# One encoder layer on one core: down projections in turn, h through DRAM everywhere, x in small pieces, paired 64-row logits

## The chip, the cores and the metric

The kernel runs on one core of a Trainium2 chip. The metric is the device time of one execution in microseconds. A core has a matrix engine (TensorE, PE in the rows, with its weight loads as PEld), a vector engine (VectorE, DVE), a scalar engine (ScalarE, ACT), a general engine (GpSimd, POOL) and a sync engine (SyncE, SP) that here issues most DMAs. Matrix results land in PSUM banks of 128 partitions by 512 fp32; everything else is held in SBUF, and weights come from device memory.

## What is computed

256 tokens of width 2048 go through one layer; all weights are fp32. The parts that the change touches are the two SwiGLU feed-forward blocks, the differential attention and the token indexer:

```python
x <- LN(alpha*x + 0.5*SwiGLU_1(x))
x <- LN(alpha*x + W_o[g_A*(DiffAttn(x) W_A) + g_B*(DSA(x) W_B)])
x <- LN(alpha*x + MemCrossAttn(x, mem))
x <- LN(alpha*x + 0.5*SwiGLU_2(x))

def _swiglu(x, w_gate, w_up, w_down):            # 2048 -> 5632 -> 2048
    return (jax.nn.silu(x @ w_gate) * (x @ w_up)) @ w_down
logits = einsum('bthcd,bshcd->bhcts', q, k)      # DiffAttn: 8 heads, c = 2 components of 64
attn = p[:, :, 0] - lam * p[:, :, 1]
head_scores = relu(einsum('bthd,bsd->bths', iq, ik))   # indexer: 16 heads of 64
```

## The kernel before

Every fp32 operand is split into a rounded part and a remainder (`split`, lines 169 to 171: ACT casts `hi`, DVE subtracts to get `lo`), and each product is three matmuls, hi·hi, hi·lo, lo·hi (`mm3`, lines 173 to 176). Weights come in units of 128 x 1024 fp32 (512 KB, two contraction tiles of 512 columns). One unit serves two halves of the tokens (t = 0, 1), so a unit is 12 matmuls of 512 columns. `Feed` holds the plan of all units in the order of use: `load` (line 179) issues the DMA on SP's queue into one of RAW = 4 raw buffers, `split_unit` splits it into one of the slots, several units ahead of PE, and `pull` hands it to the product. `product` runs the units of one 512-column chunk into two PSUM banks (`acc`, 4 of them, taken in turn) and calls `tasks.tick()` after each unit. A task is a generator that runs to its next `yield` at each tick: smaller work is written between the units in this way, and what it writes on each engine stands in that place of the engine's queue.

`ffn` (line 484) runs over groups of FFN chunks, (0,4), (4,8) and (8,11). For each chunk it makes the gate product, `silu` on ACT, the up product, and spawns a task that forms h = 0.5·silu·up and transposes it into `hh` and `hl`. After the chunks of a group come four down products (n = 0 to 3), which take the h of the group's chunks as the stationary side, in the order of the chunks, two units to a chunk.

For all chunks but the last of an FFN the task is `h_bounced` (line 496): DVE transposes 32 x 32 blocks of h, POOL's queue issues eight small DMAs into `h_dram` and two back into `hnat`, and BOUNCE = 5 ticks later ACT and DVE split the result into `hh` and `hl`. For the last chunk, 10, it is `h_task` (line 489), which transposes with eight PE matmuls against `ident` (`blocks_T`, line 337).

At the start, two warm-up matmuls of zeros run (line 557). `x` arrives transposed in four pieces of 512 KB (`x_pieces`), which stand in the plan ahead of units 0, 2, 4 and 6 of the first gate chunk and use the raw buffers. All of the first gate product runs before the first up product.

`diff_head` makes the logits of its two components one after the other, and `index_task` those of two heads per tick: each is six matmuls on 64 rows (`logits`, and lines 791 to 799), three of 128 columns and three of 256, and the two of a pair lie in rows 0 to 63 and 64 to 127 of the array and in PSUM banks of their own (`tp`, 4 of them).

Of the kernel before, what the change touches and what calls it, by code (L numbers as in the profile page):

```python
# [16 lines left out]
P = 128  # L17
T = 256
# [27 lines left out]
BOUNCE = 5  # L46
# [38 lines left out]
class Feed:  # L85


    def __init__(self, load, split):
        self.load, self.split = load, split
        self.plan, self.nth, self.order = [], [], []  # L90
        self.loaded, self.ready = [], {}
        self.nsplit = self.pulled = 0
        self.slots = {}
        self.busy = False

    def add(self, key, src, width=UNIT, into=None, cut=1):
        self.nth.append(len(self.order))
        if into is None:
            self.order.append(len(self.plan))
        self.plan.append((key, src, width, into, cut))  # L100

    def _load(self):
        i = len(self.loaded)
        if i < len(self.plan):
            _, src, width, _, cut = self.plan[i]
            self.loaded.append(self.load(src, width, cut))
# [4 lines left out]
    def _split(self):  # L111
        i = self.nsplit
        while len(self.loaded) < min(len(self.plan), i + RAW):
            self._load()
        _, _, width, into, cut = self.plan[i]
# [7 lines left out]
        if len(self.loaded) < min(len(self.plan), self.nsplit + RAW):  # L123
            self._load()
# [26 lines left out]
def tile_encoder_layer(ctx, tc, a, out):  # L151
# [27 lines left out]
    def load(src, width, cut):  # L179
        raw = wraw.tile([P, UNIT], F32, name="raw")  # L180
        w = width // cut
        for i in range(cut):
            nc.sync.dma_start(raw[:, i * w:(i + 1) * w], src[:, i * w:(i + 1) * w])
# [4 lines left out]
    def split_unit(raw, width, into, cut, slot):  # L188
        if into is not None:
            hi, lo = into()  # L190
            raw = raw.rearrange("p (k t) -> p k t", t=T)
            w = 4 // cut
# [20 lines left out]

    def plan(w, n, kts, each=None):
        for i in range(0, len(kts), KT):
            if each is not None:
                each(i // KT)
            feed.add((w, n, kts[i][1] // KT), a[w][n, kts[i][1] // KT], cut=1 if feed.order else 2)
# [6 lines left out]

    def plan_ffn(pre, each=None):
        for c0, c1 in FFN_GROUPS:
            for c in range(c0, c1):
                plan(pre + "_w_gate", c, dense(KD), each if c == 0 else None)
# [4 lines left out]
    def x_pieces(src, box):  # L234
        def piece(i):
            def into():
                xT = box[0]
                return xT[:, 0, 4 * i:4 * i + 4, :], xT[:, 1, 4 * i:4 * i + 4, :]
            feed.add(None, a[src][:, i * 4 * T:(i + 1) * 4 * T], UNIT, into, cut=1 if feed.plan else 2)
        return piece  # L240

    xbox, membox = [None], [None]
    xp, mp = x_pieces("xT", xbox), x_pieces("memT", membox)
    plan_ffn("ffn1", lambda u: u % 2 == 0 and xp(u // 2))
# [23 lines left out]
    for n in range(4):  # L268
        plan("w_mix_out", n, dense(KD), (lambda u: u % 2 == 0 and mp(u // 2)) if n == 3 else None)
# [70 lines left out]
    def transposed(src, hi, lo, width=NCOL):  # L340

        p = blocks_T(src, width)[:, :width]
        split(hi, lo, p.rearrange("p (b t) -> p b t", t=P) if len(hi.shape) == 3 else p)

# [137 lines left out]


    def ffn(pre, pool, y, xT, sts, lead, end):

        for gi, (c0, c1) in enumerate(FFN_GROUPS):
            hT = []

            def h_task(s, u, hh, hl):
# [8 lines left out]
            def h_bounced(s, u, hh, hl):  # L498

                h = [pool.tile([P, NCOL], F32, name="hnat", bufs=3) for _ in range(2)]  # L500
                via = dram.tile([P, 2, 4, P], F32, name="h_dram", bufs=4)
                for t in range(2):
                    nc.vector.scalar_tensor_tensor(h[t], s[t], 0.5, u[t], op0=ALU.mult, op1=ALU.mult)
                yield
                for t in range(2):
                    nc.vector.transpose(s[t].rearrange("p (g b i) -> p g b i", b=4, i=32),  # L506
                                        h[t].rearrange("p (b g i) -> p g b i", b=4, i=32))
                    for q in range(4):
                        nc.gpsimd.dma_start(via[:, t, q].rearrange("(g i) c -> i g c", i=32),  # L509
                                            s[t][32 * q:32 * q + 32].rearrange("i (g c) -> i g c", g=4))  # L510
                for t in range(2):
                    nc.gpsimd.dma_start(h[t].rearrange("p (q c) -> p q c", q=4), via[:, t])
                for _ in range(BOUNCE):
                    yield
                for t in range(2):
                    sl = slice(t * P, (t + 1) * P)
                    split(hh[:, :, sl].rearrange("p b (q j) -> p b q j", j=32),
                          hl[:, :, sl].rearrange("p b (q j) -> p b q j", j=32),
                          h[t].rearrange("p (q b j) -> p b q j", b=4, j=32))

            for c in range(c0, c1):
                g = product(x_lhs(xT), pre + "_w_gate", c, dense(KD), lead=lead if c == 0 else 0)
                s = [pool.tile([P, NCOL], F32, name="silu", bufs=2) for _ in range(2)]
                for t in range(2):
                    nc.scalar.activation(s[t], g[t], AF.Silu)
                u = product(x_lhs(xT), pre + "_w_up", c, dense(KD))
# [11 lines left out]
            for n in range(4):  # L538
# [13 lines left out]
    with more_slots("wx1", MORE[0]), tc.tile_pool(name="ffn1", bufs=1) as pool:  # L552
# [6 lines left out]
        xT = xbox[0] = new_xT()  # L559
# [597 lines left out]
```

## Time and profile before

| | us |
|---|---|
| median of three runs | 2259.17 (2258.37 to 2260.03) |
| the profiled execution, its own time | 2260.71 |
| its span, first to last instruction | 2258.9 |
| PE busy | 2237.8, 99% of the span, 10248 matmuls |
| DVE, ACT, POOL busy | 1308.0, 1035.9, 131.5 |
| DMA | 458.26 MB, mean 203 GB/s |
| mean granted clock of TensorE | 0.998 |

A busy PE is counted from the start of a matmul to its modelled end, and neighbouring matmuls overlap: 512-column matmuls last 0.39 us by the record and start 0.23 us apart. Lost PE time is therefore read from the distance between starts, not from the busy share. In a timeline each row gives the start, the time covered, engine, line, operation, written and read tiles, shapes and count; the bracket gives the engine's idle time before it and what ended that.

### The profile page before, as it was taken

Reading aid. Unit: us, or ns where it says so; the run is one execution under the profiler, and the core shown is the slowest. Engines: PE = TensorE matmul, PEld = TensorE weight load, DVE = VectorE, ACT = ScalarE, POOL = GpSimd, SP = SyncE. Lnnn points to the kernel's source line nnn. Section 1 sums busy time; section 2 is a strip of 40 time slices with the busy share of each in tenths; the row PEclk is TensorE's granted clock in tenths of the full one; section 3 lists DMA queues with packets and bytes.
Section 4 is the critical chain, followed back from the end, with each engine's and each line's share of the span. In section 5 each row is a group of like instructions: output and inputs, shape, how many; then the busy total and the mean of one; then the engine's idle time right before and its main releaser. Section 6 shows DMA issues by size and latency. Waiting matters only on the chain.

```text
span 2258.9 us, 27277 instructions
## 1 busy us (share of the span) xinstructions
PE 2237.8 (99%) x10248; PEld 1850.0 (82%) x10248; DVE 1308.0 (58%) x1498; ACT 1035.9 (46%) x1317; POOL 131.5 (6%) x236
## 2 busy tenths in 40 slices
PE   9999999999999999999999999999999999999997
PEld 7888888888888888888888888878888888888886
DVE  6555555554556666685655556777555455554554
ACT  5443344444443555655544444655444344434442
POOL 0100000100000000000000000000000001100100
PEclk9999999999999999999999999999999999999999
DMA  8877677766665655445567667557776666766762
GB/s 272 315 236 212 190 210 215 213 207 195 212 209 168 209 159 165 151 147 170 183 193 207 202 224 263 174 168 227 221 251 207 194 213 212 230 192 191 221 198 91
DMA packets 128916, 458.26 MB, mean 203 GB/s; under 512 B 16704, under 2 KB 16832, under 8 KB 127632
## 3 DMA queue, kind: packets, MB, share of 16 engines
q1 hardware_dynamic: 119520, 431.02, 62.2%
q0 software_dynamic: 9264, 25.51, 3.4%
q8 instruction: 80, 1.31, 0.2%
q14 instruction: 52, 0.43, 0.1%
HBM read 441.78 MB, written 14.68 MB: 202 GB/s over the span
## 4 chain that ended last, share of the span: by engine, by line
PE 94%; DMA 2%; issue 1%; DVE 1%; ACT 1%; POOL 0%; POOLq 0%; SPq 0%; DVEq 0%; ACTq 0%
PE acc L174 30%; PE acc L176 30%; PE acc L175 30%; PE tp L337 2%; DMA hnat<-h_dram 1%; DMA h_dram<-silu 1%; PE tp L174 1%; PE tp L175 1%; PE tp L176 0%; DMA raw<-in_ffn_w_gate 0%; ACT whi L170 0%; DVE wlo L171 0%; POOL h_dram L509 0%; DVE y L479 0%; ACT me L1010 0%
## 5 line engine op out<-in xcount | busy, mean ns | idle before, releaser
L171 DVE TENSOR_TENSOR wlo<-raw,whi 128x1024 fp32r<-128x1024 f32 (+1 forms) x787 | 958.3, 1222 | 811.3 <-ACT whi L170 808.7
L170 ACT CAST whi<-raw 128x1024 fp32r<-128x1024 f32 (+1 forms) x787 | 824.1, 1051 | 932.5 <-PE acc L176 874.2
L174 PE MATMUL acc<-whi,xT 128*128 128x512 f32 x2176 | 853.8, 392 | 1.7 <-ACT whi L170 1.7
L176 PE MATMUL acc<-whi,xT 128*128 128x512 f32 x2176 | 848.3, 390 | 0.0
L175 PE MATMUL acc<-wlo,xT 128*128 128x512 f32 x2176 | 848.2, 390 | 0.0
L174 PEld LDWEIGHTS acc<-whi,xT 128*128 128x128 f32 x2176 | 409.2, 188 | 87.1 <-ACT whi L170 3.3
L176 PEld LDWEIGHTS acc<-whi,xT 128*128 128x128 f32 x2176 | 409.0, 188 | 86.0
L175 PEld LDWEIGHTS acc<-wlo,xT 128*128 128x128 f32 x2176 | 409.4, 188 | 84.4 <-DVE wlo L171 0.9
L174 PE MATMUL acc<-whi,hh 128*128 128x512 f32 x704 | 274.9, 390 | 2.3 <-ACT hh L170 2.3
L176 PE MATMUL acc<-whi,hl 128*128 128x512 f32 x704 | 274.4, 390 | 0.0
L175 PE MATMUL acc<-wlo,hh 128*128 128x512 f32 x704 | 274.0, 389 | 0.0
L174 PEld LDWEIGHTS acc<-whi,hh 128*128 128x128 f32 x704 | 132.1, 188 | 30.9 <-ACT hh L170 4.0
L176 PEld LDWEIGHTS acc<-whi,hl 128*128 128x128 f32 x704 | 132.1, 188 | 29.1 <-DVE hl L171 1.7
L175 PEld LDWEIGHTS acc<-wlo,hh 128*128 128x128 f32 x704 | 132.2, 188 | 27.3
L509 POOL DMA_DIRECT2D h_dram<-silu x160 | 87.2, 553 | 1077.0 <-DVE silu L506 1027.2
L174 PE MATMUL acc<-whi,ring 128*128 128x512 f32 x144 | 56.7, 394 | 0.0
L176 PE MATMUL acc<-whi,ring 128*128 128x512 f32 x144 | 56.1, 390 | 0.0
L175 PE MATMUL acc<-wlo,ring 128*128 128x512 f32 x144 | 56.1, 389 | 0.0
L479 DVE SCALAR_TENSOR_TENSOR y<-y,acc 128x512 f32<-128x512 f32 x64 | 42.2, 679 | 17.3 <-PE acc L176 17.3
L669 ACT ACTIVATE e<-e,nm 128x128 f32<-128x128 f32 (+1 forms) x48 | 21.5, 448 | 45.7 <-DVE nm L668 44.8
L170 ACT CAST hh<-hnat 128x512 fp32r<-128x512 f32 x40 | 24.8, 621 | 37.7 <-DMA hnat<-h_dram 34.8
L171 DVE TENSOR_TENSOR hl<-hnat,hh 128x512 fp32r<-128x512 f32 x40 | 27.4, 691 | 25.2 <-ACT hh L170 25.2
(200 smaller groups left out, 1136.6 us busy)
## 6 DMA issues: line engine op xcount, KB each, us to landing
raw<-in_ffn_w_up SPq DMA_DIRECT2D x176, 512.0 KB, 4.4
raw<-in_ffn_w_down SPq DMA_DIRECT2D x176, 512.0 KB, 4.2
raw<-in_ffn_w_gate SPq DMA_DIRECT2D x175, 512.0 KB, 4.3
raw<-in_w_in SPq DMA_DIRECT2D x88, 512.0 KB, 3.6
raw<-in_w_gate SPq DMA_DIRECT2D x64, 512.0 KB, 4.1
raw<-in_w_mix_out SPq DMA_DIRECT2D x32, 512.0 KB, 4.4
h_dram<-silu POOLq DMA_DIRECT2D x160, 64.0 KB, 4.4
hnat<-h_dram POOLq DMA_DIRECT2D x40, 256.0 KB, 5.3
```

The source lines that it names most:

```text
L170: nc.scalar.copy(hi, src)
L171: nc.vector.tensor_tensor(lo, src, hi.bitcast(F32), ALU.subtract)
L174: nc.tensor.matmul(dst, lh, rh, start=start, stop=False)
L175: nc.tensor.matmul(dst, lh, rl, start=False, stop=False)
L176: nc.tensor.matmul(dst, ll, rh, start=False, stop=stop)
L337: nc.tensor.transpose(p[:, b * P:(b + 1) * P], src[:, b * P:(b + 1) * P], ident)
L479: nc.vector.scalar_tensor_tensor(c, c, scale, d, op0=ALU.mult, op1=ALU.add)
L509: nc.gpsimd.dma_start(via[:, t, q].rearrange("(g i) c -> i g c", i=32), s[t][32 * q:32 * q + 32].rearrange("i (g c) -> i g c", g=4))
L669: nc.scalar.activation(e[:, s0:s1], e[:, s0:s1], AF.Exp, bias=nm[:, t:t + 1], accum_out=sm[:, t:t + 1])
```

## The change

- The units of the first two down products of a group are put in turn: first, for n = 0 and n = 1, the units of all chunks but the group's last, then the last chunk's units for both. Products 2 and 3 follow as before. The four PSUM banks are held by the two products together.
- The h of every chunk, the last too, goes through DRAM; BOUNCE is 6 ticks.
- `x` comes in eight pieces of 256 KB, one for each pair of units; they land in the tile `y` and not in the raw buffers, the first two by ACT's DMA queue. Gate and up of the first FFN chunk are run unit by unit in turn (`first_products`), and the two first units of each are loaded and split in halves.
- The logits of the two halves of the rows are issued matmul by matmul in turn (`twin_logits`), in the differential heads and in the indexer.

```diff
-BOUNCE = 5
+BOUNCE = 6
     def _load(self):
-        i = len(self.loaded)
-        if i < len(self.plan):
+        while len(self.loaded) < len(self.plan):
+            _, src, width, _, cut, lands = self.plan[len(self.loaded)]
+            if lands is None and self.raw == RAW:
+                return
+            self.raw += lands is None
+            self.loaded.append(self.load(src, width, cut, *(lands() if lands else (None,))))
...
+    def down_order(c0, c1):
+        early, nu = 2 * (c1 - c0 - 1), 2 * (c1 - c0)
+        return [(n, i) for part in (range(early), range(early, nu)) for n in range(2) for i in part]
...
+                if each is not None and c == 0:
+                    for u in range(KD // KT):
+                        each(u)
+                        for w in ("_w_gate", "_w_up"):
+                            plan_unit(pre + w, c, u, 2 if u < 2 else 1)
+                    continue
...
+    def x_piece(i):
+        def into():
+            xT, _ = xbox[0]
+            return xT[:, 0, 2 * i:2 * i + 2, :], xT[:, 1, 2 * i:2 * i + 2, :]
+        def lands():
+            at = xbox[0][1].rearrange("p t d -> p (t d)")[:, i * 2 * T:(i + 1) * 2 * T]
+            return at, (nc.scalar if i < 2 else nc.sync)
+        feed.add(None, a["xT"][:, i * 2 * T:(i + 1) * 2 * T], 2 * T, into, 1 if i else 2, lands)
...
+    def first_products(lhs, ws, after):
+        dst = [[acc() for _ in range(2)] for _ in ws]
+        nu = KD // KT
+        for i in range(nu):
+            for w, d in zip(ws, dst):
+                u = feed.pull((w, 0, i))
+                if i == 0:
+                    hi, lo = u[0]
+                    for j in range(KT):
+                        c = slice(j * NCOL, (j + 1) * NCOL)
+                        for n, (side, rhs) in enumerate(((0, hi), (1, hi), (0, lo))):
+                            for t in range(2):
+                                nc.tensor.matmul(d[t], lhs(j, t)[side], rhs[:, c], start=j == n == 0, stop=False)
+                else:
+                    for t in range(2):
+                        unit_mm(lhs, d, u, [i * KT + j for j in range(KT)], t, False, i == nu - 1)
+                feed.free(u)
+                if w == ws[0] and i == nu - 1:
+                    after(d)
+                tasks.tick()
+        return dst
...
-                for t in range(2):
-                    sl = slice(t * P, (t + 1) * P)
-                    transposed(h[t], hh[:, :, sl], hl[:, :, sl])
...
+                turn([(h[t], s[t], h[t]) for t in range(2)])
                 for _ in range(BOUNCE):
                     yield
...
-                tasks.spawn((h_task if c == DFF // NCOL - 1 else h_bounced)(s, u, hh, hl))
+                tasks.spawn(h_task(s, u, hh, hl))
...
-            for n in range(4):
+            d = [[acc() for _ in range(2)] for _ in range(2)]
+            for n, i in down_order(c0, c1):
+                u = feed.pull((pre + "_w_down", n, 2 * c0 + i))
+                for t in range(2):
+                    unit_mm(h_lhs, d[n], u, [2 * i, 2 * i + 1], t, i == 0, i == 2 * (c1 - c0) - 1)
+                    if i == 2 * (c1 - c0) - 1:
+                        add_chunk(y, t, n, d[n][t], 1.0 if gi else ALPHA, sts if final else None)
+                feed.free(u)
+                tasks.tick()
+            for n in range(2, 4):
...
+        def twin_logits(q, blk, key):
+            p = [tp(), tp()]
+            for t, (s0, s1) in enumerate(SEG):
+                ts_ = slice(t * P, (t + 1) * P)
+                for i, (a, b) in enumerate(((0, 0), (0, 1), (1, 0))):
+                    for half in range(2):
+                        rowsl = slice(half * 64, half * 64 + 64)
+                        nc.tensor.matmul(p[half][:, s0:s1], q[rowsl, a, blk, ts_], key(rowsl, b, slice(s1 - s0)),
+                                         start=i == 0, stop=i == 2)
+            return p
...
-            for c in range(2):
-                es.append(softmax_exp(distm, slope, logits(q, k, slice(c * 64, c * 64 + 64), b)))
+            es = [softmax_exp(distm, slope, p) for p in twin_logits(q, b, lambda r, h, c: k[r, h, b, c])]
...
+            for h in range(0, 16, 2):
+                pls = twin_logits((iq0, iq1)[h // 8], h % 8 // 2, lambda r, i, c: ikT[r, i, c])
+                for half, pl in enumerate(pls):
```

`turn` is the bounce of `h_bounced`, written for any pair of tiles: the DVE transposes and the ten DMAs on POOL's queue are the same, in the same order, into tiles of 256 KB of which there are six.

## Rows read from the trace of the kernel before

**Rows 1.** The page's chain that ended last, shares of the span by engine.
```profile
PE 94%; DMA 2%; issue 1%; DVE 1%; ACT 1%; POOL 0%; POOLq 0%; SPq 0%; DVEq 0%; ACTq 0%
```
**Rows 2.** Waits of PE: us in total, times, longest.
```profile
PE acc L174 <- ACT hh L170: 2.3, 4, 0.6
```
**Rows 3.** Timeline of PE over one pair of indexer heads.
```profile
952.83 0.39 PE L176 MATMUL acc<-whi,xT 128*128 128x512 f32 x1
953.15 0.33 PE L174 MATMUL tp<-ikT,ring 64*128 64x128 f32 x1
953.32 0.27 PE L175 MATMUL tp<-ikT,ring 64*128 64x128 f32 x1
953.42 0.27 PE L176 MATMUL tp<-ikT,ring 64*128 64x128 f32 x1
953.43 0.43 PE L174 MATMUL tp<-ikT,ring 64*128 64x128 f32 x2
...
954.11 0.27 PE L176 MATMUL tp<-ikT,ring 64*128 64x256 f32 x1
954.31 0.50 PE L174 MATMUL acc<-whi,xT 128*128 128x512 f32 x1
```
**Rows 4.** Groups of PE by line and form, 64-row matmuls: busy us, mean ns, idle.
```profile
L174 PE MATMUL tp<-ring 64*128 64x256 f32 x16 | 4.9, 331 | 0.0
L174 PE MATMUL tp<-ikT,ring 64*128 64x256 f32 x16 | 4.9, 329 | 0.0
```
**Rows 5.** Timeline of PE where the first group's last h is first used.
```profile
200.23 0.39 PE L176 MATMUL acc<-whi,hl 128*128 128x512 f32 x1
201.20 0.50 PE L174 MATMUL acc<-whi,hh 128*128 128x512 f32 x1 [0.58 <-ACT hh L170]
201.53 0.40 PE L175 MATMUL acc<-wlo,hh 128*128 128x512 f32 x1
```
**Rows 6.** Timeline of ACT ahead of the same place.
```profile
195.21 1.05 ACT L170 CAST whi<-raw 128x1024 fp32r<-128x1024 f32 x1 [1.67 <-PE acc L176]
197.93 1.05 ACT L170 CAST whi<-raw 128x1024 fp32r<-128x1024 f32 x1 [1.67 <-PE acc L176]
200.53 0.62 ACT L170 CAST hh<-hnat 128x512 fp32r<-128x512 f32 x1 [1.54 <-DMA hnat<-h_dram]
```
**Rows 7.** Timeline of PE at the PE transposes of the last chunk, first FFN.
```profile
667.73 0.39 PE L176 MATMUL acc<-whi,hl 128*128 128x512 f32 x1
667.96 1.03 PE L337 MATMUL tp<-ident,hnat 128*128 128x128 f32 x8
668.75 0.48 PE L174 MATMUL acc<-whi,hh 128*128 128x512 f32 x1
669.06 0.39 PE L175 MATMUL acc<-wlo,hh 128*128 128x512 f32 x1
```
**Rows 8.** Timeline of all engines over the first 40 us.
```profile
0.73 1.28 ACT L170 ACT_TABLE_LOAD   x1 [0.73 <-PEq L1149]
0.74 0.86 SPq L183 DMA_DIRECT2D raw<-in_xT  x2
...
1.46 3.78 PE L557 MATMUL acc<-hnat 128*128 128x512 f32 x4 [1.46 <-DVE hnat L554]
...
3.97 1.29 ACT L170 CAST xT<-raw 128x512 fp32r<-128x512 f32 x2 [1.95 <-DMA raw<-in_xT]
...
6.26 0.62 ACT L170 CAST whi<-raw 128x512 fp32r<-128x512 f32 x1 [1.00 <-DMA raw<-in_ffn_w_gate]
...
6.93 0.79 PE L174 MATMUL acc<-whi,xT 128*128 128x512 f32 x1 [1.69 <-ACT whi L170]
...
8.67 0.63 PE L174 MATMUL acc<-whi,xT 128*128 128x512 f32 x1
...
12.51 0.63 PE L174 MATMUL acc<-whi,xT 128*128 128x512 f32 x1
...
13.22 0.39 PE L176 MATMUL acc<-whi,xT 128*128 128x512 f32 x1
```

More of the change, by code (lines that the diff above doesn't have):

```diff
@@ L217, in plan @@
                 each(i // KT)
-            feed.add((w, n, kts[i][1] // KT), a[w][n, kts[i][1] // KT], cut=1 if feed.order else 2)
+            plan_unit(w, n, kts[i][1] // KT)
     def dense(ks):
@@ L343, in transposed, with turn, in_order, groups @@
         split(hi, lo, p.rearrange("p (b t) -> p b t", t=P) if len(hi.shape) == 3 else p)
+    def turn(tiles):
+        vias = []
+        for src, way, _ in tiles:
+            via = dram.tile([P, 4, P], F32, name="via", bufs=6)
+            nc.vector.transpose(way.rearrange("p (g b i) -> p b g i", b=4, i=32),
+                                src.rearrange("p (b g i) -> p b g i", b=4, i=32))
+            for q in range(4):
+                nc.gpsimd.dma_start(via[:, q].rearrange("(g i) c -> i g c", i=32),
+                                    way[32 * q:32 * q + 32].rearrange("i (g c) -> i g c", g=4))
+            vias.append(via)
+        for (_, _, dst), via in zip(tiles, vias):
+            nc.gpsimd.dma_start(dst.rearrange("p (q c) -> p q c", q=4), via)
+    def in_order(x):
+        return x.rearrange("p (q b j) -> p b q j", b=4, j=32)
+    def groups(x):
+        return x.rearrange("p b (q j) -> p b q j", j=32)
     def new_xT():
@@ L516, in h_bounced, with silu @@
                     sl = slice(t * P, (t + 1) * P)
-                    split(hh[:, :, sl].rearrange("p b (q j) -> p b q j", j=32),
-                          hl[:, :, sl].rearrange("p b (q j) -> p b q j", j=32),
-                          h[t].rearrange("p (q b j) -> p b q j", b=4, j=32))
+                    split(groups(hh[:, :, sl]), groups(hl[:, :, sl]), in_order(h[t]))
             for c in range(c0, c1):
[L522 to L526, printed above, removed]
+                s = []
+                def silu(g):
+                    for t in range(2):
+                        s.append(pool.tile([P, NCOL], F32, name="silu", bufs=2))
+                        nc.scalar.activation(s[t], g[t], AF.Silu)
+                if first and c == 0:
+                    u = first_products(x_lhs(xT), (pre + "_w_gate", pre + "_w_up"), silu)[1]
+                else:
+                    silu(product(x_lhs(xT), pre + "_w_gate", c, dense(KD), lead=lead if c == 0 else 0))
+                    u = product(x_lhs(xT), pre + "_w_up", c, dense(KD))
                 hh = pool.tile([P, 4, T], F32R, name="hh", bufs=4)
                 hl = pool.tile([P, 4, T], F32R, name="hl", bufs=4)
-                tasks.spawn((h_task if c == DFF // NCOL - 1 else h_bounced)(s, u, hh, hl))
+                tasks.spawn(h_task(s, u, hh, hl))
                 hT.append((hh, hl))
```

96 lines of the change are left out of this document (36 added, 60 removed).

## The prediction, made before the changed kernel was run

> **What bounds the kernel now.** Read the chain that ended last first: 94% of it is PE [rows 1]. The reader is to see that no other engine and no queue sets the pace, so an edit is worth what it takes off PE's own row of starts, and an edit on ACT, DVE or a queue is worth nothing unless PE waits for it. Next the waits of PE: the only one inside the FFNs is for `hh`, four times, 2.3 us in all [rows 2]. That view counts only the time in which no matmul was running; matmuls overlap, so the real loss is taken from the distances between starts. An ordinary 512-column matmul starts 0.23 us after the one before it [rows 7], and ACT's casts of weight units, which follow PE, are 2.72 us apart [rows 6], the time of one unit of twelve. The timelines then show the four places that the change touches: a pair of 64-row logits, the group ends, the PE transposes, the start.
>
> **Twin logits.** From the last ordinary matmul ahead of a pair to the first behind it is 952.83 to 954.31 = 1.48 us; less the ordinary 0.23, a pair holds PE for 1.25 us [rows 3]. There are 16 pairs: 16 first matmuls of the 256-column form for the indexer and 16 for the differential heads, two to a pair [rows 4]. The starts inside the pair run from 953.15 to 954.11, 0.96 us. The first head alone goes at steps of 0.17 and then 0.10 us; then at 953.43, 0.01 us after the start at 953.42, a matmul of the second head starts (it is still one of 128 columns, of which the first head has only three), and from there the two heads run beside each other [rows 3]. So the two row halves do work at once, but the second one joins 0.28 us late, and at the end it runs alone. Issued in turn, both halves start together, and twelve matmuls take six steps: 0.17 + 4 x 0.11 = 0.61 us from the first start to the last, up to 0.05 us more if the second of each pair follows a little later (half of the 0.11 step). Gain per pair 0.96 - 0.61 = 0.35, or 0.30 with that lag; I take 0.33, and 16 x 0.33 = 5.3 us (bounds 4.8 to 5.6). All of it is PE's own time, so nothing hides it. Both `tp` banks must now be free at the first matmul, not the second one 0.28 us later; four exist, and I see no wait ahead of a pair (0.32 us to its first start, of which 0.23 is the ordinary step). Edges outside: the halves no longer overlap when issued in turn, and 12 x 0.11 = 1.3 us of starts make each pair 0.35 slower, 5.6 us in all; or all 1.25 us are halved, a rival below.
>
> The Trainium skill, "TensorEngine Tiling (Array Packing)", section Theoretical Speedup, gives up to 2x where the contraction is at most 64 rows. The trace shows a pair that already overlaps for about half of its length, so the part still to be won is smaller than that rule suggests.
>
> **Down products in turn, h of the last chunk.** At the first group's end the step 200.23 to 201.20 is 0.97 us and the next 0.33 us, where 0.23 each is ordinary: 0.74 + 0.10 = 0.84 us lost [rows 5]. Four such places are counted [rows 2], the two groups of four chunks in each FFN: 3.4 us. ACT stood 1.54 us waiting for the DMA of h before its cast at 200.53 [rows 6], so the round trip through DRAM sets this. In the old order the last chunk's h is due after six units, 6 x 2.72 = 16.3 us from the end of the up product; it came 0.74 us later, at 17.1 us. In the new order it is due after 12 units, 32.6 us, so the wait goes, and nothing else is late there: weight casts wait for PE, 1.67 us before each [rows 6], so they have room.
>
> In the third group h is made with eight PE transposes: 667.73 to 669.06 is 1.33 us where two ordinary steps would be 0.46, so 0.87 us, in two FFNs 1.7 us [rows 7]. With DRAM the h is due after two times four units, 8 x 2.72 = 21.8 us; it takes 17.1 us now with BOUNCE 5. BOUNCE 6 moves its cast behind one more weight cast, 1.05 us on ACT [rows 6], so about 18 us for the first half and 19.5 us for the second. Cover 2 to 3.5 us; if it is used up, every us late costs one us at each of two places. The ten DMAs stand on POOL's queue, where nothing else waits then, and behind the waiting cast on ACT stand weight casts for units that are several units away. I take the whole 3.4 + 1.7 = 5.1 us (bounds 3.4, with the two last groups gaining nothing, to 5.3). Holding all four `acc` banks costs nothing: the second product's banks are those of the up product, read when h is formed, and are first written four or six units later.
>
> **The start.** The first real matmul starts at 6.93 us, after ACT waited for the first gate half and cast it in 0.62 [rows 8]. Ahead of that half stood 512 KB of x: two issues of 0.43 us each from 0.74 on, and both halves cast by 3.97 + 1.29 = 5.26. Now 256 KB of x in two issues on ACT's queue and 256 KB of gate on SP's are needed, together as much as the x alone before, whose second cast began at about 3.97 + 0.65 = 4.6. With 0.62 for the cast the first matmul starts at about 5.3 to 5.9. If the table load of 1.28 us [rows 8] stands ahead of ACT's DMA issues, or its issue (none is in this trace) is slow, it is up to 6.6. I take 5.7.
>
> The matmuls up to 12.51 last 0.63 us and are (12.51 - 8.67) / 9 = 0.427 us apart; at 13.22 they last 0.39, with 0.23 between them [rows 8]: PE ran at 1.2 GHz and then at 2.4, the rise at about 13.1. The four warm-up records end at 5.24, and then PE stood 1.69 us. A us in the slow stretch loses 1 - 0.23/0.427 = 0.46 us. Lateness of the stream before: 6.93 + 0.46 x 6.2 = 9.8 us. After: if the slow run is as long, 5.7 + 2.85 = 8.55, a gain of 1.2; if the rise stays at 13.1, 5.7 + 0.46 x 7.4 = 9.1, a gain of 0.7; if there were no slow stretch at all, 4.1. The gap behind the warm-up nearly closes, which speaks for an earlier rise, so I take 1.4 (bounds 0, with a first matmul at 6.6 and a slightly later rise, to 4.1). Later x pieces do not stall it: gate and up in turn need 256 KB of x and two units per 5.44 us (1.25 MB) where the old order needed 1.5 MB. The silu of the first gate now has one unit, 2.72 us, before its banks are written again; with a table load of 1.28 and 0.6 for the first half it is done, and cover left is 0.8 us, once.
>
> The Trainium skill, "Trainium Kernel Development and Optimization", section Key Constraints, says that DMAs of SP, ACT and POOL share the same 16 engines and that several issuers save issue time only. By that rule the second queue for x is worth no more than the two or three issues of 0.43 us in the rows, and the smaller first pieces must do the rest; the start term above hangs on bytes in the same way.
>
> **The sum.** 5.3 + 5.1 + 1.4 = 11.8 us. The profiled execution took 2260.71 us (span 2258.9, so 1.8 us lie around it), which gives 2248.9; it was 1.5 us above the median of the runs, 2259.17, and the median so becomes 2247.4 us, 0.5% less. The bounds together, 4.8 + 3.4 + 0 = 8.2 and 5.6 + 5.3 + 4.1 = 15.0, give 2244.2 to 2251.0.
>
> **Rivals.**
> - The pairs gain nothing, since the overlap is there already and the array's real limit is the weight loads, one for each matmul. For: one half alone steps at 0.11 us for 128 as for 256 columns. Against: the two halves' starts lie 0.01 us apart. 2259.17 - 6.5 = 2252.7.
> - The pairs halve, edges included, with two full streams that share the array: 16 x 0.625 = 10.0 us in place of 5.3. Against: the steps into and out of a pair (0.32 and 0.20 us) are not shared. 2242.7. (The 2x of the Trainium skill, "TensorEngine Tiling (Array Packing)", section Theoretical Speedup, is this case.)
> - The turn-taking ends the overlap (the edge above, 5.6 us worse): 2259.17 + 5.6 - 6.5 = 2258.3, no change.
> - Slower: the DRAM trip of the last chunk takes longer than its cover. It decides from 21.8 us on, in the two third groups; PE idles for the excess, and ACT's weight casts stand behind the late cast. To lose by over 0.2% it needs (11.8 + 4.5) / 2 = 8.2 us of excess at each, a trip of 30 us where 17.1 was seen. With 8.5: 2264.4. Nothing in the rows points that way.
> - The start does not change (the clock or the queues eat it): 2248.8, inside the range.
>
> **How the numbers follow.** Forecast with the start's variants 0.77; pairs without gain 0.10; pairs halved 0.06; overlap ended 0.04; slower 0.03. The range must leave out at most 2 in 10: 2243.0 to 2252.7 takes in the forecast's bounds and the first rival, 0.87, and leaves the others out. About 0.2%, 4.5 us, is what a measurement of this kernel can tell from no change. Faster by more than that: forecast, first two rivals, 0.93; within: 0.04; slower: 0.03.
>
> **What would show it.** In the timeline of PE, a pair of logits with 0.6 to 0.66 us from first to last start and all starts in twos; no wait for `hh` in PE's waits; no `ident,hnat` transposes near the down products; the first gate matmul before 6 us and 0.39-us matmuls before 13 us. Wrong would be: starts inside a pair still 0.9 us apart, a wait for `hh` in the third groups, or a new wait of PE behind the first silu.

## The result, and the profile after

The changed kernel takes 2246.82 us (median of four runs, 2246.36 to 2247.54). Run beside it, the kernel before took 2258.77 (2257.25 to 2260.03). The ratio is 0.9949, 95% interval 0.9935 to 0.9963: faster by 0.5%, 12.0 us. A second comparison on another chip gave 2246.22 against 2258.91, ratio 0.9941 (0.9929 to 0.9954).

The profiled execution of the changed kernel took 2246.47 us with a span of 2244.7, so its span is 14.2 us shorter than that of before. That is 2.3 us more than the medians differ: the profiled execution of before was a long one, 1.94 us over the median of this comparison, and that of after was 0.35 us under its median.

The page of the changed kernel, busy time by engine and the chain that ended last by engine (compare [rows 1]):

```profile
PE 2227.4 (99%) x10232; PEld 1844.6 (82%) x10232; DVE 1307.0 (58%) x1509; ACT 1034.5 (46%) x1324; POOL 142.4 (6%) x256
PE 98%; DVE 1%; issue 1%; ACT 0%; DMA 0%; POOL 0%; POOLq 0%; ACTq 0%
```

PE still sets the pace. It has 16 matmuls fewer, the eight transposes of each last chunk's h. The waits of PE in the changed kernel (total us, times, longest):

```profile
PE tp L364 <- ACT y L516: 5.5, 2, 4.1
...
PE acc L546 <- ACT whi L173: 1.1, 1, 1.1
PE tp L364 <- ACT ring L173: 0.8, 1, 0.8
```

The row for `hh` [rows 2] is gone, the wait ahead of the first gate matmul is 1.1 in place of 1.7 us, and the last row is new: the attention's latents now arrive behind PE (below).

Where the 14.27 us of PE's starts and of the end went is read by laying the two timelines of PE side by side, from one landmark to the next. A landmark is a matmul that both kernels have, with the same work ahead of it:

| stretch | shorter by, us | predicted |
|---|---|---|
| to the first down matmul of the first group | 1.94 | 1.4 |
| four ends of groups of four chunks | 4.69 (1.18, 1.20, 1.15, 1.16) | 3.4 |
| last group of the first FFN | 0.92 | 0.87 |
| mixer, all 16 pairs of logits | 3.85 | 5.3 |
| LayerNorm near 1520 us | 0.37 | 0 |
| last group of the second FFN to PE's last start | 1.36, of it 0.87 the group | 0.87 |
| behind PE's last start | 1.14 | 0 |

Some of this is chance of the two profiled executions and no work of the change. At the LayerNorm, which the change does not touch, PE waits 1.6 us before and 1.2 after; in eleven of the twelve other executions profiled below it waits 1.2 to 1.3. In the last stretch 0.45 us is the program's last eight transposes, of the final LayerNorm: 2.71 us from the first start to the last before, all at a granted clock of 0.50 (1.2 GHz), and 2.26 after, where the first four still ran at 1.00. Of the eight other executions with the last h through DRAM, five have 2.71 as well. The four group ends were long in this trace of before, too (below).

The pairs first, in PE's timeline of the changed kernel (start us, time covered, engine, line, operation, tiles, count):

```profile
945.35 0.39 PE L179 MATMUL acc<-whi,xT 128*128 128x512 f32 x1
945.67 0.95 PE L740 MATMUL tp<-ikT,ring 64*128 64x128 f32 x12
946.54 0.50 PE L177 MATMUL acc<-whi,xT 128*128 128x512 f32 x1
...
968.63 0.95 PE L740 MATMUL tp<-ikT,ring 64*128 64x128 f32 x12
969.50 0.66 PE L364 MATMUL tp<-ident,nat 128*128 128x128 f32 x4
970.95 0.63 PE L364 MATMUL tp<-ident,nat 128*128 128x128 f32 x4 [0.79 <-ACT ring L173]
```

From the last ordinary matmul ahead of a pair to the first behind it is now 946.54 - 945.35 = 1.19 us where it was 1.48 [rows 3]. The group row of twelve hides the single starts; taken one by one, the second head's matmul starts 0.003 us after the first head's, and first to last is 0.67 to 0.68 us. The last two rows are the new wait: four transposes of the first half of the latents, then 0.79 us of nothing, then four of the second half.

The first use of the first group's last h, in the same timeline (before: [rows 5]):

```profile
214.60 0.39 PE L179 MATMUL acc<-whi,hl 128*128 128x512 f32 x1
214.83 0.39 PE L177 MATMUL acc<-whi,hh 128*128 128x512 f32 x1
215.06 0.39 PE L178 MATMUL acc<-wlo,hh 128*128 128x512 f32 x1
```

Every step is 0.23 us, and the last h is first used at 214.83, 32.6 us after the group's first down matmul at 182.19. Its cast of the third group, in ACT's timeline of the changed kernel:

```profile
677.43 1.05 ACT L173 CAST whi<-raw 128x1024 fp32r<-128x1024 f32 x1 [1.67 <-PE acc L179]
678.38 1.14 ACT L173 CAST hh<-hnat 128x512 fp32r<-128x512 f32 x2
680.19 1.05 ACT L173 CAST whi<-raw 128x1024 fp32r<-128x1024 f32 x1 [0.67 <-ACT hh L173]
```

The two casts stand in one row and wait for nothing. They end at 679.52, 18.6 us after the up product's end at 660.91, and PE wants them at 682.67: 3.1 us of cover.

The start, all engines (before: [rows 8]):

```profile
0.74 1.37 ACTq L186 DMA_DIRECT2D y<-in_xT  x3
...
2.14 1.28 ACT L173 ACT_TABLE_LOAD   x1 [2.14 <-issue]
...
4.39 0.40 ACT L173 CAST xT<-y 128x256 fp32r<-128x256 f32 x1 [0.96 <-DMA y<-in_xT]
...
5.36 0.40 ACT L173 CAST xT<-y 128x256 fp32r<-128x256 f32 x1 [0.57 <-DMA y<-in_xT]
5.67 1.13 ACT L173 CAST whi<-raw 128x512 fp32r<-128x512 f32 x2
...
6.34 2.07 PE L546 MATMUL acc<-whi,xT 128*128 128x512 f32 x4 [1.10 <-ACT whi L173]
```

The first gate half had landed at 4.19 us, but ACT works in order: it stood for the second half of x until 5.36 and cast it before the gate half. So the first matmul starts at 6.34, not at 5.7.

The end, in the view of the groups of the program's last line (POOL's and SP's queue, which have three DRAIN instructions each at that line; the three numbers are ns, shortest, median, longest of three; then the start of the first and of the last), of the kernel before and of the changed one:

```profile
L1153 POOLq DRAIN  x3: 40/102/9862, 2248.3 to 2258.7; - x3
L1153 SPq DRAIN  x3: 7/7/7, 2256.8 to 2258.4; - x3
```
```profile
L1228 POOLq DRAIN  x3: 40/93/2837, 2235.6 to 2244.4; - x3
L1228 SPq DRAIN  x3: 7/7/7, 2243.8 to 2244.1; - x3
```

POOL's first DRAIN of the program's end took 9.86 us before and 2.84 after. Before, it began at 2248.29 and ended at 2258.15, 1.31 us behind SP's second DRAIN (2256.84), and SP's last one stands behind it, at 2258.4; after, POOL is through 5 us ahead of SP. No part of the change is aimed at this.

### The profile page after: what moved, and what is told of

Its sections match the earlier page's. It is cut to its first block, busy times and chain, and to the rows that moved or that the text cites. A ratio compares the mean times of both kernels' runs of the same rounds, so it can differ in the third digit from the quotient of the medians.

```text
span 2244.7 us, 27322 instructions
## 1 busy us (share of the span) xinstructions
PE 2227.4 (99%) x10232; PEld 1844.6 (82%) x10232; DVE 1307.0 (58%) x1509; ACT 1034.5 (46%) x1324; POOL 142.4 (6%) x256
## 3 DMA queue, kind: packets, MB, share of 16 engines
q8 instruction: 80, 1.31, 0.2%
## 4 chain that ended last, share of the span: by engine, by line
PE 98%; DVE 1%; issue 1%; ACT 0%; DMA 0%; POOL 0%; POOLq 0%; ACTq 0%
PE acc L177 31%; PE acc L179 31%; PE acc L178 31%; PE tp L364 1%; PE tp L740 1%; PE tp L179 0%; PE tp L177 0%; PE acc L546 0%; PE tp L178 0%; DMA y<-in_xT 0%; DVE wlo L174 0%; ACT whi L173 0%; ACT me L1085 0%; DVE nm L1081 0%; POOL rstd L358 0%
## 5 line engine op out<-in xcount | busy, mean ns | idle before, releaser
L382 POOL DMA_DIRECT2D via<-silu x176 | 95.9, 553 | 1140.9 <-DVE silu L379 1052.4
L580 ACT ACTIVATE silu<-acc 128x512 f32<-128x512 f32 x44 | 26.0, 598 | 19.7 <-PE acc L179 19.7
L179 PEld LDWEIGHTS acc<-whi,ring 128*128 128x128 f32 x144 | 27.0, 188 | 5.7
```

The source lines that it names most:

```text
L179: nc.tensor.matmul(dst, ll, rh, start=False, stop=stop)
L382: nc.gpsimd.dma_start(via[:, q].rearrange("(g i) c -> i g c", i=32), way[32 * q:32 * q + 32].rearrange("i (g c) -> i g c", g=4))
```

## Experiments

Theories at this point: the three parts act one by one at PE's starts, as the prediction has it (pairs, turn and DRAM, start); the latents' wait comes from PE arriving sooner at a chain of fixed length; the start hangs on what stands ahead of the first gate cast. Rivals: the parts act through something common; the wait is for a PSUM bank; the start is a matter of PE's clock only. A gain below is against the median of the kernel before in the same comparison, 2258.39, 2258.91, 2258.52 or 2258.5.

**Twin logits alone.** The kernel before with `twin_logits` in both places:

```diff
-                es.append(softmax_exp(distm, slope, logits(q, k, slice(c * 64, c * 64 + 64), b)))
+            es = [softmax_exp(distm, slope, p) for p in twin_logits(q, b, lambda r, h, c: k[r, h, b, c])]
...
```

> The kernel before with the paired logits alone. Theory: the pair's first-to-last start falls from 0.96 to 0.67 or 0.68 us as in the changed kernel, 16 pairs save 4.5 us, and 0.6 us comes back at one place, where the PE transposes of the latents wait for VectorE after the last pairs (in the changed kernel the step there is 1.06 us, before 0.42). Net 3.9 us, 2254.9 us against 2258.8. Rival: the gain of 3.9 us between the first mixer product and the first gate of branch A has other causes, and the pairs alone give under 2 us.

Measured 2255.83, ratio 0.9986 (0.9977 to 0.9996). By the timelines the mixer is 3.92 us shorter, as in the full change, with the latents' wait there too (0.7 us, below). The median gains 2.6, and its interval, 0.9 to 5.2, takes in the 3.9 expected; the rival's "under 2" is ruled out by the rows, not by the medians. The rest of its profiled execution tells how much the other places vary by themselves: the four group ends, not changed here, lost 1.36, 0.49, 0.12 and 0.90 us. The latents' row among the waits of PE in this kernel:

```profile
PE tp L337 <- DVE nat L833: 0.7, 1, 0.7
```

**Down products in turn and h through DRAM alone.** The order of units, BOUNCE = 6 and the bounce for the last chunk; x and logits as before:

```diff
-            for n in range(4):
+            for n, i in down_order(c0, c1):
+                plan_unit(pre + "_w_down", n, 2 * c0 + i)
+            for n in range(2, 4):
...
```

> The kernel before with the down products in turn and the h of every chunk through DRAM with BOUNCE 6, nothing else. Theory: the four group ends of four chunks give 1.17 us each (0.75 for hh and 0.16 for hl, each followed by a step of 0.11 too long, and one more of 0.11), the two groups of three chunks 0.9 us each: 6.5 us, 2252.3 us. Rival: part of that comes with the other start or the pairs, and this alone gives the 5.1 us that was predicted, 2253.7.

Measured 2252.56, ratio 0.9974 (0.9964 to 0.9984), a gain of 5.8 us (3.6 to 8.1, which does not tell the 6.5 expected from the rival's 5.1). No wait for `hh` is left among PE's waits. By the stretches, against the profiled execution of before, the four group ends gain 1.18, 1.20, 1.15 and 1.16, the last group of the first FFN 0.89, and the end behind PE's last start 1.28: POOL's DRAIN is 2.83 us here.

**The start alone.** x in pieces and gate and up in turn; the rest as before:

```diff
-    plan_ffn("ffn1", lambda u: u % 2 == 0 and xp(u // 2))
+    plan_ffn("ffn1", x_piece)
...
```

> The kernel before with x in small pieces and gate and up of the first chunk in turn, nothing else. Theory: the first gate matmul at 6.3 us in place of 6.9; from the first group's down products on everything is 0.6 to 1.9 us earlier, depending on when TensorE goes from 1.2 to 2.4 GHz (before at 13.0 us, changed kernel at 9.9). 2257.0 to 2258.2 us. Rival: the clock's rise follows the first matmul by a fixed time, then the gain is the 0.6 us of the first matmul alone.

Measured 2256.42, ratio 0.9989 (0.9979 to 0.9998), a gain of 2.0 us; first matmul at 6.38, first down matmul at 182.07, 2.06 earlier than before, a little over the 0.6 to 1.9 expected, so by the rows the rival's 0.6 falls. Its four group ends lost 0.85, 1.15, 1.03 and 0.61. The small pieces of x and the order of gate and up in turn went in together; which of them gives how much is not shown. The three medians add to 2.6 + 5.8 + 2.0 = 10.4 us, the whole gives 12.0 and 12.7: within what their intervals allow, so there is no sign of a common cause or of one part eating another.

**The latents' transposes one tick later.** The full change with one more `yield` ahead of them:

```diff
             yield
+            yield
             for t in range(2):
                 s = slice(t * P, (t + 1) * P)
                 transposed(c[t], cT[:, 0, :, s], cT[:, 1, :, s])
```

> The changed kernel with one more yield ahead of the PE transposes of the latents, which are then written one unit later. Theory: the wait of 0.8 us there (PE for the latents' VectorE chain) is a fixed chain that PE now reaches too soon; one unit later it is ready, the step of 1.06 us falls to 0.11, and the time falls by 0.9 us, to 2245.9 against 2246.8 of the changed kernel. Rival: the wait is for a free PSUM bank behind the relu of the pairs; then it moves with the transposes and stays.

Measured 2244.33, ratio 0.9938 (0.9924 to 0.9953), a gain of 14.1 us where the changed kernel has 12.0 and 12.7; it was not run beside it. The mixer's stretch is now 4.82 us shorter than before, 0.97 more than with the full change. PE at that place, in the kernel before and here:

```profile
978.95 1.43 PE L337 MATMUL tp<-ident,nat 128*128 128x128 f32 x8
```
```profile
972.86 0.95 PE L740 MATMUL tp<-ikT,ring 64*128 64x128 f32 x12
973.73 1.09 PE L364 MATMUL tp<-ident,nat 128*128 128x128 f32 x8
```

Eight transposes in one go, right behind a pair and with the same four banks: a bank that was missing would be missing here too, so that rival falls. They also take 0.34 us less than before, where PE already waited a little in their midst: the fifth started 0.42 us after the fourth, and 0.11 is ordinary. The row that the second four waited for in the changed kernel is DVE's last write of `nat`, which ends at 970.80, followed by PE at 970.95:

```profile
970.05 0.75 DVE L903 SCALAR_TENSOR_TENSOR nat<-acc,rc,kvg 128x512 f32<-128x512 f32 x1 [0.67 <-POOL rc L358]
```

The view of the waits names ACT's `ring` for this wait, but that cast ends at 970.955, just behind PE's start. PE starts 0.15 us after DVE's row in each of the executions that have the wait, the twin logits alone and the kernel before among them. The chain is one of ACT, DVE, POOL and DVE again, whose part from DVE on takes 3.05 us before (976.56 to 979.61) and after (967.75 to 970.80), and the twin logits, standing between the task's start and the transposes, bring PE to its end sooner.

**The changed kernel again**, as a reference on the chip of the next experiments:

> The changed kernel again, beside the two that follow, so that differences under 2 us can be read on one chip: 2246 to 2247 us. The clock's rise to 2.4 GHz lies anywhere between 8 and 13 us, as in the runs so far (9.6, 9.9, 10.4 with this start).

Measured 2246.22, ratio 0.9941 (0.9929 to 0.9954).

**x in two pieces around the first gate unit.** The first piece of x is cut in two entries of 128 KB, and the second stands behind the first gate unit in the plan, and so in ACT's order:

```diff
-                        each(u)
-                        for w in ("_w_gate", "_w_up"):
-                            plan_unit(pre + w, c, u, 2 if u < 2 else 1)
+                        if u:
+                            each(2 * u, 2)
+                        else:
+                            each(0, 1)
+                        plan_unit(pre + "_w_gate", c, u, 2 if u < 2 else 1)
+                        if u == 0:
+                            each(1, 1)
+                        plan_unit(pre + "_w_up", c, u, 2 if u < 2 else 1)
...
```

> The changed kernel, but the first x piece is two plan entries of 128 KB with the first gate unit between them, so that ACT casts the first gate half (landed at 4.2 us) ahead of the second x half (5.3). Theory: the first matmul starts at about 5.4 us in place of 6.3, since ACT no longer waits there; at 1.2 GHz that is worth 0.5 us, and up to 2 us if the rise of the clock comes earlier with the gap behind the warm-up closed. Rival: the gate half then waits for its DMA as well, 0.2 us or nothing.

Measured 2244.37, ratio 0.9936 (0.9923 to 0.9948), 1.9 us under the changed kernel in the same comparison. The first matmul starts at 5.35, PE is fast from its first real matmul, and the first down matmul comes at 179.60. (The LayerNorm near 1504 us lost 1.09 us more in that execution; the medians have it or not as it comes.)

**x around the gate unit and the latents later,** the two diffs above together:

> The split of the first x piece around the gate unit and the later latents together. Theory: the two add, 0.5 to 2 us at the start and 0.95 us at the latents: 2244 to 2245.3 us where the changed kernel has 2246.8. Rival: one of the two only moves the wait, then under 0.5 us.

Measured 2243.43, ratio 0.9932 (0.9920 to 0.9945): 2.8 us under the changed kernel beside it (2246.22) and the fastest version here. The two add: 1.9 us by the run above and 0.97 at the latents by the rows. Its start:

```profile
1.46 3.76 PE L631 MATMUL acc<-hnat 128*128 128x512 f32 x4 [1.46 <-DVE hnat L628]
...
4.27 0.41 ACT L173 CAST xT<-y 128x256 fp32r<-128x256 f32 x1 [0.85 <-DMA y<-in_xT]
4.58 1.13 ACT L173 CAST whi<-raw 128x512 fp32r<-128x512 f32 x2
...
5.25 1.20 PE L551 MATMUL acc<-whi,xT 128*128 128x512 f32 x4
...
5.62 0.40 ACT L173 CAST xT<-y 128x256 fp32r<-128x256 f32 x1
```

The gate cast now stands between the two x casts. The warm-up ends at 1.46 + 3.76 = 5.22 and the first real matmul starts at 5.25; its four take 1.20 us where the changed kernel's took 2.07.

**The same without the warm-up matmuls.** What the closed gap is worth, and whether it is the early data or the clock:

```diff
-WARM = 2
+WARM = 0
```

> The kernel with the split first x piece and the later latents, without the two warm-up matmuls. With them TensorE went to 2.4 GHz at 5.1 us, just ahead of the first matmul at 5.25, and stayed. Theory: the rise needs the work ahead of it; without it the first matmul still starts at about 5.3 us, the rise comes 3 us or more later, and each of these costs 0.46 us: 1.5 to 3 us slower than with the warm-up, 2245 to 2246.5. Rival: the rise does not depend on the warm-up; then the time stays at 2243.4.

Measured 2245.23, ratio 0.9940 (0.9923 to 0.9956). PE's start:

```profile
5.32 2.07 PE L551 MATMUL acc<-whi,xT 128*128 128x512 f32 x4 [5.32 <-ACT whi L173]
```

The data come at the same time, but the first four matmuls take 2.07 us, not 1.20, the slow ones go on until 10.57, and the first down matmul comes at 181.99 in place of 179.47: 2.5 us later, at one execution each (the ratios differ by 0.0008, 1.8 us). So with x around the gate unit, most of the gain over the changed kernel is the clock that the warm-up has already brought up. What the warm-up is worth in the changed kernel, with its gap of 1.1 us, was not run.

**The first x pieces on SP's queue** in the changed kernel, with the gate halves behind them:

```diff
-            return at, (nc.scalar if i < 2 else nc.sync)
+            return at, nc.sync
```

> The changed kernel with its first two x pieces issued on SP's queue like the others. Theory: two issues of 0.43 us now stand ahead of the first gate half on SP, which is issued at 1.6 us in place of 0.74 and lands 0.5 to 0.9 us later than 4.2; the first matmul starts at about 6.8 in place of 6.3 us, 0.2 to 0.5 us in all. Rival: the bytes decide and not the issues, then the first matmul stays at 6.3.

My own theory expected a later start here and was wrong. Measured 2244.72, ratio 0.9938 (0.9918 to 0.9958), where the changed kernel had 0.9949 and 0.9941: not slower. The start:

```profile
2.97 0.81 ACT L173 CAST xT<-y 128x256 fp32r<-128x256 f32 x2 [0.95 <-DMA y<-in_xT]
...
5.31 0.62 ACT L173 CAST whi<-raw 128x512 fp32r<-128x512 f32 x1 [1.54 <-DMA raw<-in_ffn_w_gate]
...
5.98 1.20 PE L546 MATMUL acc<-whi,xT 128*128 128x512 f32 x4 [0.93 <-ACT whi L173]
```

x lands at 2.95 and 3.35 and the two gate halves at 5.29 and 6.12; with two queues the gate halves came at 4.19 and 5.16, x at 4.36 and 5.34. The three pieces that ACT casts up to the first matmul are in by 5.3 either way; the second queue only changed which of them comes last. All four were in by 5.34 with two queues and by 6.12 with one, 0.8 us later, where the fourth was issued at 2.12 and not at 1.18, 0.9 us later. The Trainium skill, "Trainium Kernel Development and Optimization", section Key Constraints, has the queues share one set of DMA engines, so that several issuers save issue time only; these landings agree with that. That this kernel is ahead of the changed one in its ratio says little of the queue: PE was fast from its first real matmul in the profiled execution (table below).

**BOUNCE = 5** in the changed kernel, to see if the sixth tick does anything:

> The changed kernel with BOUNCE 5 in place of 6. Theory: ACT waits 1 to 1.6 us for the DMA ahead of its casts of h again, as in the kernel before, but in the new order h is due six units later (two in the third groups), so PE still has no wait for hh and the time stays at 2246 to 2247. Rival: the waits of ACT hold up weight casts that PE needs, then PE shows waits for whi in the groups' down products.

Measured 2247.09, ratio 0.9948 (0.9929 to 0.9968): no difference from the changed kernel that can be told. The row of h among ACT's waits:

```profile
ACT hh L173 <- DMA hnat<-via: 39.3, 40, 2.8
```

ACT now waits ahead of 40 of its 44 casts of h for the DMA that brings h back, up to 2.8 us; in the changed kernel that row is 0.2 us, once. PE has no wait for `hh` in either. The tick takes a wait off an engine that has the time anyway.

**The last chunk's h by PE transposes again**, in the changed kernel; the order in turn stays:

```diff
-                tasks.spawn(h_task(s, u, hh, hl))
+                tasks.spawn((h_last if c == DFF // NCOL - 1 else h_task)(s, u, hh, hl))
...
```

> The changed kernel, but the h of the last chunk of each FFN is transposed by eight PE matmuls again, as before the change; the units stay in turn. Theory: 0.9 us on PE at each of two places, 1.8 us slower than the changed kernel, 2248.6, since nothing hides them. Rival: the DRAM trip of the third group costs somewhere what it saves; then the time stays at 2246.8.

Measured 2248.52, ratio 0.9955 (0.9941 to 0.9968), 2.3 us above the changed kernel beside it. PE at the place of [rows 7], and the program's end:

```profile
661.96 1.03 PE L364 MATMUL tp<-ident,hnat 128*128 128x128 f32 x8
```
```profile
L1237 POOLq DRAIN  x3: 40/102/9860, 2235.8 to 2246.1; - x3
```

0.87 us come back at each of two places, and POOL's DRAIN is back at 9.86 us and ends 1.16 us behind SP's part of the end: 2 x 0.87 + 1.16 = 2.9 beside 2.3 by the medians. (The profiled executions differ by 1.6 only, since this one began early, with its first down matmul at 180.51 and not 182.32.) So sending the last h through DRAM is worth about 1.7 us on PE, as predicted, and 1.2 us at the end that nobody counted.

**A late DMA on POOL's queue in the kernel before**, to see if the DRAIN is short where POOL has issued a DMA recently:

```diff
+                    if pre == "ffn2":
+                        nc.gpsimd.dma_start(pool.tile([P, 8], F32, name="scrap"), a["ident"][:, :8])
```

> The kernel before with one small DMA more on POOL's queue (128 x 8 values of the identity into a tile that nothing reads), issued ahead of the very last down product. In every run so far the program's last DRAIN on POOL takes 9.86 us where POOL's last DMA lies over 100 us back (kernels whose last h goes over PE) and 2.84 us where it lies under 70 us back (last h through DRAM); with 9.86 it ends 1.3 us after SP has done its part, so the span ends later. Theory: what counts is how long ago POOL's last DMA was, so this one short DMA brings the DRAIN to about 2.8 us and the time to 2257.2 against 2258.5. Rival: the length depends on something else that the changed kernel has (ten more DMAs in each FFN), then the DRAIN stays at 9.86 and the time at 2258.5.

Measured 2258.95, ratio 1.0002 (0.9992 to 1.0012): no change. POOL's timeline, and the end:

```profile
2144.29 0.53 POOL L542 DMA_DIRECT2D scrap<-in_ident  x1
```
```profile
L1156 POOLq DRAIN  x3: 40/102/9942, 2246.5 to 2256.9; - x3
```

The experiment missed its aim. POOL had nothing to wait for and issued that DMA at 2144.29, 102 us ahead of the DRAIN, just as far as the last one of before (2146.23). So neither the theory nor the rival was put to the test. Over all runs, the DRAIN takes 9.86 to 9.94 us in the kernels whose last chunk does not go through POOL's queue (before, the first and third experiments, the PE transposes, this one; 213 or 214 DMAs by POOL) and 2.83 or 2.84 us in the nine whose last chunk does (233 DMAs). Whether the number of DMAs, the time of the last one or something else decides is open.

**What the start varies by.** From the profiled executions, at the same 64 units of work ahead of the last column (times in us):

| kernel | first real matmul | matmuls of 0.39 to 0.50 us | first down matmul |
|---|---|---|---|
| before | 6.93 | from 13.0 | 184.13 |
| twin alone | 6.92 | until 8.5, again from 15.3 | 185.60 |
| turn alone | 7.62 | from 11.0 | 183.58 |
| late POOL DMA | 7.06 | until 9.2, again from 12.6 | 184.20 |
| changed | 6.34 | from 9.9 | 182.19 |
| changed, again | 6.36 | from 10.1 | 182.32 |
| start alone | 6.38 | from 9.6 | 182.07 |
| latents later | 6.59 | from 10.4 | 182.58 |
| BOUNCE = 5 | 6.22 | from 10.3 | 182.29 |
| PE transposes | 6.28 | from the first | 180.51 |
| x on SP | 5.98 | from the first | 180.20 |
| x around gate | 5.35 | from the first | 179.60 |
| both | 5.25 | from the first | 179.47 |
| both, no warm-up | 5.32 | from 10.6 | 181.99 |

Old start 184.4 on average (four), the change's start 182.0 (six, with the one that was fast from the first): 2.4 us.

## Why the prediction came out as it did

The forecast was 2247.4 us, the measurement 2246.8, and the likeliest case, all three parts gaining, is what happened. The sum of 11.8 us stands beside 12.0 by the medians. Its terms fared less evenly than that, and the closeness of the sum is in part luck: the pairs gave 1.4 us less than their term, the start and the end of the program 1.6 to 2.2 more.

- **Pairs: mechanism right, size too high, and a cover not looked at.** Both halves start in twos, 0.003 us apart, and first to last takes 0.67 to 0.68 us, not 0.61 to 0.66. The step in "0.17 + 4 x 0.11" that failed: the long first step of 0.165 comes twice, once at the first 128-column matmul and once at the first of 256. A pair gains 0.283 us, 16 of them 4.5 in place of 5.3. And 0.64 us of it were given back at the latents, where PE now arrives ahead of the data. The prediction looked for a wait ahead of a pair and not for one behind it; "all of it is PE's own time, so nothing hides it" left out what PE then meets. With one tick more the stretch gains 4.82: the pairs and the 0.31 us that PE waited at the latents in the kernel before already. The rivals "no gain", "overlap ended" and "halved, edges included" fell: a pair holds PE for 1.19 - 0.23 = 0.96 us, where it was 1.25. The Trainium skill, "TensorEngine Tiling (Array Packing)", section Theoretical Speedup, has up to 2x for at most 64 rows; here it is 1.3x, over a pair that overlapped in part already [rows 3].
- **Group ends: right, a term too small.** The loss at each was put at 0.74 + 0.10 us, and the profiled execution gained 1.15 to 1.20. The prediction read two steps and stopped. Right behind the two, from 201.53 on [rows 5], PE waits again, for `hl`, which DVE makes behind ACT's cast. From the kernel before:

```profile
201.92 0.50 PE L176 MATMUL acc<-whi,hl 128*128 128x512 f32 x1
202.26 0.40 PE L174 MATMUL acc<-whi,hh 128*128 128x512 f32 x1
```
```profile
201.18 0.69 DVE L171 TENSOR_TENSOR hl<-hnat,hh 128x512 fp32r<-128x512 f32 x1 [0.93 <-ACT hh L170]
```

  DVE ends at 201.87, and the steps 201.53 to 201.92 and 201.92 to 202.26 are 0.16 and 0.11 over 0.23. But one execution is a sample: the four places together lost 4.69, 2.87, 3.64 and 3.19 us in the four profiled executions with the old order (before, twin alone, start alone, late POOL DMA), 3.6 on average, beside the 3.4 predicted. Two errors nearly cancel by luck, the missed step and a trace that showed a bad draw.
- **Third groups: right.** 0.87 predicted, 0.92 and 0.87 in the rows, 0.87 back at each place with the PE transposes. The h was expected after 18 to 19.5 us and was there after 18.6, with 3.1 us of cover ("2 to 3.5"). The rival of a late trip never came near.
- **The start: more than its term, and by another way.** The term was 1.4 us; the rows have 1.9, the averages above 2.4. The first matmul was to come at 5.7 and came at 6.34. "Needed, together as much as the x alone before" overlooked ACT's order: the gate half, there at 4.19, waited behind the cast of an x half that landed at 5.34. ACT's table load was no matter, as it came behind the issues and was over at 3.42. What made up for it is the rise, at 9.9 and not 13.1: by the prediction's own formula 6.34 + 0.46 x 3.5 = 7.95 against 6.93 + 0.46 x 6.1 = 9.74, a gain of 1.8 (1.94 in the rows). "No slow stretch at all, 4.1" came true with x around the gate unit: 184.13 - 179.60 = 4.5 us.
- **The end: not seen.** The view of the chain starts from the last instruction that counts as work, which ended at 2254.2, 4.7 us ahead of the span's end, and the 9.86 us of POOL's DRAIN stood in before's trace. Costing an edit on POOL's queue at nothing, "where nothing else waits then", was right for the queue and missed 1.1 to 1.2 us of gain at the program's end, whose cause is open.

## What to carry to other kernels

Where one engine is busy 94% of the chain, read the distances between its starts at the place of each wait until they are ordinary again: the first late operand is often followed by a second one made from it. An edit that makes the bound engine faster moves it against chains of fixed length behind the edit, so look for the next thing that it will meet and give that one a step more room. Data that lands early is of no use if the engine that prepares it has something that lands later ahead of it in its order.

## What the runs showed of the hardware

The column of the granted clock does not tell of the slow matmuls at a program's start. A table by stretch, of the kernel before and of the twin logits alone (stretch, length, busy time and count of PE, PEld, DVE, ACT and POOL, then the granted clock, DMA share, GB/s):

```profile
10.00:12.00 2.00, 2.00 (x6) 1.60 (x5) 1.95 (x2) 1.79 (x2) 0.00 (x0) 1.00 0.83 283
```
```profile
6.00:8.00 2.00, 0.85 (x3) 0.49 (x3) 0.69 (x1) 0.62 (x1) 0.00 (x0) 1.00 0.93 347
...
10.00:12.00 2.00, 2.00 (x6) 1.52 (x6) 1.42 (x2) 1.57 (x2) 0.00 (x0) 0.50 0.74 201
```

From 10 to 12 us six matmuls run in both kernels, nearly all of them 0.63 us long (before: [rows 8]), but only the second table says 0.50, 1.2 GHz; the first says 1.00 throughout. In the first, the clock had not yet risen when the slow matmuls ran; in the second it had risen and fell again. So I take the level at the start from the matmuls' durations, and the second table confirms that 0.63 us is the lower level. PE's rows of the twin logits alone show the fall:

```profile
6.92 0.50 PE L174 MATMUL acc<-whi,xT 128*128 128x512 f32 x1 [1.71 <-ACT whi L170]
...
7.99 0.40 PE L176 MATMUL acc<-whi,xT 128*128 128x512 f32 x1
...
10.65 0.63 PE L174 MATMUL acc<-whi,xT 128*128 128x512 f32 x1
...
15.33 0.40 PE L176 MATMUL acc<-whi,xT 128*128 128x512 f32 x1
```

PE was fast at 6.92 to 8.5, after 1.71 us without a matmul, and slow from then to 15.3. That the same start code gives a first down matmul between 183.6 and 185.6, and the changed start one of 180.5 to 182.6, is mostly this: when the level rises differs from execution to execution. In the two executions where the gap behind the warm-up was under 0.25 us (x around the gate unit, with and without the later transposes) it was high from the first; with the gaps of 0.9 to 1.4 us of the seven others with the change's start and a warm-up, it was so in two.

The second finding is POOL's DRAIN, told above. The third is that matmuls on different row halves of the array overtake: in the old pairs a 128-column matmul of the second head starts at 953.43, 0.01 us behind the third of the first head's 128-column ones [rows 3], and ahead of that head's three of 256 columns, which the kernel issues ahead of it; the first of them starts at 953.54.
